# Mixer B's weights: 32x32 boxes turned by VectorE and placed through DRAM, in place of transposes on TensorE

## The chip, the cores and the metric

The kernel runs on one core of one Trainium2 chip. The metric is the device time in microseconds (us) of one execution, from start to end on that core; a lower time is better. Engines are named as the profile names them: PE (TensorE, matrix products), PEld (its loads of the stationary operand), DVE (VectorE), ACT (ScalarE), POOL (GpSimd) and SP (SyncE, which only issues DMAs; SPq is its queue).

## What is computed

One step of a layer with two attention mixers that work side by side on the same projection. 128 prompt tokens and 1024 latent tokens (eight tiles of 128) are normalized, projected and given rotary positions. Mixer A lets each latent token attend to all latent keys and 128 cached context keys. Mixer B lets it attend to the keys at most 128 places away, to the context keys, and to a learned sink per head. Each mixer has 8 query heads in two groups of four that share one key and value head of 64. The outputs are multiplied by SiLU gates, joined, and put through one output projection. What the change touches is mixer B for latent tokens:

```python
def window_attn_latent(q, k_lat, v_lat, k_ctx, v_ctx, sink):
    ...
    s_band = jnp.einsum('bnqkgd,bnskd->bnkgqs', qb, kband).astype(jnp.float32) * scale
    ...
    valid = (jnp.abs(rel)[None] <= WINDOW) & (abs_j >= 0) & (abs_j < n)
    s_band = jnp.where(valid[None, :, None, None], s_band, NEG_INF)
    s_ctx = jnp.einsum('bnqkgd,bskd->bnkgqs', qb, k_ctx).astype(jnp.float32) * scale
    ...
    s = jnp.concatenate([sink_column(sink, kv, s_ctx.shape[:-1]), s_ctx, s_band], axis=-1)
    p = jax.nn.softmax(s, axis=-1).astype(v_lat.dtype)
    ...
    o = (jnp.einsum('bnkgqs,bskd->bnqkgd', p_ctx, v_ctx)
         + jnp.einsum('bnkgqs,bnskd->bnqkgd', p_band, vband))
```

All of it is in float32. The kernel gets that precision from TensorE's fast format by splitting an operand into a high part and a low part, the rest that rounding left over, and adding the products.

## The kernel before

Projection, gates and keys come first; the last 400 us or so are the attention stage, and the change lies in it alone. The stage goes through 36 *units* in order: for latent tiles t = 1 to 8, for both groups g of heads, first mixer A (m = 0), then mixer B (m = 1); at the end four units of the prompt. An A unit and the B unit behind it are called a pair here.

Each unit is cut into *slots*, one for each block of 128 keys: nine for an A unit (context and eight tiles), and for a B unit four (the tile before, the context, the tile itself, the tile after; three for tiles 1 and 8, which lack a neighbour). The main loop at the end of the kernel takes the slots in order. In each, it first runs what was put on an agenda with `later(n, f)` (do f n slots from now), then `scores` of the slot's block, then what was due at this slot by plan (`put`), then two or three steps of the output projection, and last `values` of the block that is LAG = 3 slots back. `in_order` makes this written order the order of every engine's queue, SyncE's among them: an instruction that waits holds up all that stands behind it on its engine.

In an A unit, `scores` computes a block's scores already turned, keys on the partitions (L1316, L1317: bank st), ScalarE takes the exponential (L1319, pe) and its high part (L1323, ph), GpSimd or VectorE the low part (pl, L1327 or L1325). `values` multiplies both with the values (L1337, L1339, L1340: bank pv). The maxima that the exponentials need were found by L985 and L986 (pmx, mx).

A B unit i needs its scores with queries on the partitions, since the window's mask and the maximum go along the keys. `weight_items` does this early: in slots 0 to 3 of the A unit ahead, one head per slot, two matmuls (L1066, L1067: bank sn) and a VectorE instruction (L1070) that adds the mask and takes the minimum of the negated scores; one slot later ScalarE's exponential (L1056) writes the head's 128 x 512 weights to the tile `pen`. The weights are not divided; the sum's inverse is folded into the gates later (`sinks`, `total`, `divide`, `turned`, `put`, `rows`). `pen` has one buffer.

For `values` the weights have to be turned, keys on the partitions. In the B unit's slots, `scores` does this with four transposes on TensorE for each block (L1311, bank st), then ScalarE's copy (L1312, ph) and VectorE's subtraction (L1313, pl). For tiles 2 to 7 (`paired`) blocks 0 and 3 share one group of four transposes, because the window masks of the two leave complementary triangles: `pair` merges block 3 into block 0 (L1017 on VectorE) and leaves block 3 its diagonal (L1018 on GpSimd), the slot before the unit starts `unpair` turns the merged block (L1030, bank st_pair) and takes block 0 out of it (L1032), and `unpair_rest` takes out block 3 (L1036). Blocks 0 and 3 then get their high part from SBUF (L1304, ScalarE) and their low part on GpSimd (L1305).

SyncE's queue in a pair holds, in this order (slots counted from the start of the A unit): the rows of inverse sums of the pair before (L1134, slot 0), in every other pair a store of y (L1435, about slot 2), a gate (L1291, sgl) and a query tile (L965, qt) in slot 4, again a store of y, a gate and a query tile in slot 8, the inverse sums (L1129) and a query tile's part (L990, qb) in slot 10, and in the pairs that come before a store of y two loads of yt.

Of the kernel before, what the change touches and what calls it, by code (L numbers as in the profile page):

```python
# [12 lines left out]
I16 = mybir.dt.int16  # L13
# [6 lines left out]
P = 128  # L20
# [56 lines left out]
PAIR_AT = 2  # L77
# [40 lines left out]
def hybrid_step(ctx, tc, x_prompt, x_sample, cache_k_a, cache_v_a, cache_k_b, cache_v_b,  # L118
# [11 lines left out]
    gate_row = dram.tile([2, D], F32, name="gate_row")  # L130
    r_dram = [dram.tile([4, P], F32, name=f"rd{i}") for i in range(2 * NL)]
# [877 lines left out]
    divided = {}  # L1009

    def paired(t):

        return 1 < t < NL

    def pair(i):
        prev, nxt = (penat[i][:, :, o : o + P] for o in (0, 3 * P))
        nc.vector.copy_predicated(prev, mask[:, 0:P].bitcast(I16).unsqueeze(1).to_broadcast([P, 4, P]), nxt)  # L1017
        nc.gpsimd.affine_select(out=nxt, in_=nxt, pattern=[[0, 4], [-1, P]], compare_op=ALU.is_equal, fill=0.0, base=0,  # L1018
                                channel_multiplier=1)

    shared = {}

    def unpair(i):

        divided.pop(i)()
        prev = penat[i][:, :, 0:P]
        over = mask[:, 3 * P : 4 * P].unsqueeze(1).to_broadcast([P, 4, P])
        s = bank("B", f"st{i}_pair")
        for h in range(4):
            nc.tensor.transpose(s[:, P * h : P * h + P], prev[:, h], ident_r.bitcast(F32))  # L1030
        shared[i] = s.rearrange("p (h n) -> p h n", h=4)
        nc.vector.scalar_tensor_tensor(prev, over, 0.0, shared[i], op0=ALU.is_ge, op1=ALU.mult)  # L1032

    def unpair_rest(i):
        over = mask[:, 3 * P : 4 * P].bitcast(I16).unsqueeze(1).to_broadcast([P, 4, P])
        nc.vector.copy_predicated(penat[i][:, :, 3 * P : 4 * P], over, shared.pop(i))  # L1036

    def weight_items(i):
# [7 lines left out]
        def first(n):  # L1046
            if t:
                penat[i] = qp2[0].tile([P, 4, 512], F32, tag="pen", name=f"pen{i}")[:, :, 0:n]
            else:
                penat[i] = w3.tile([P, 512], F32, tag="pe", name=f"pen{i}", bufs=PES).rearrange(  # L1050
                    "p (h n) -> p h n", h=4)
# [3 lines left out]
        def exp(h, s, scale):  # L1055
            nc.scalar.activation(penat[i][:, h], s, AF.Exp, bias=v["nm"][:, h : h + 1], scale=scale,  # L1056
                                 accum_out=v["sum"][:, h : h + 1])

# [28 lines left out]
        def finish():  # L1087
            nc.gpsimd.tensor_tensor(v["ex"], v["nm"], sink[:, 4 * g : 4 * g + 4], op=ALU.add)
            if paired(t):
                later(PAIR_AT, lambda: pair(i))  # L1090
            if paired(t):
                later(EX_AT[0], sinks)
                later(EX_AT[1], total)
                divided[i] = divide
            elif t:
# [13 lines left out]
        def divide():  # L1109
# [6 lines left out]
            o = int(paired(t))  # L1116
            later(ROWS_AT[0] + o, turned)
            later(ROWS_AT[1] + o, put)
            later(ROWS_AT[2] + o, rows)
            later(ROWS_AT[3] + o, lambda: nc.gpsimd.tensor_tensor(sgl[i], sgl[i], v["rows"], op=ALU.mult))  # L1120
# [176 lines left out]
    def scores(i, b, blk):  # L1297
# [3 lines left out]
        if m == 1 and paired(t) and blk[0] in (0, 3):  # L1301
            p = penat[i][:, :, P * blk[0] : P * blk[0] + P]
            ph4, pl4 = (a.rearrange("p (h n) -> p h n", h=4) for a in (ph, pl))
            nc.scalar.copy(ph4, p)  # L1304
            nc.gpsimd.tensor_tensor(pl4, p, ph4, op=ALU.subtract)  # L1305
            return ph, pl
# [23 lines left out]
    def values(i, b, last, blk, ph, pl):  # L1330
# [15 lines left out]
        def inverse():  # L1346
            if t:
                v["rs"] = w2.tile([64, 512], F32, tag="rs", name=f"rs{i}", bufs=1)
            else:
                if not rs_prompt:  # L1350
                    rs_prompt.append(qp2[0].tile([P, 4, 512], F32, tag="pen", name="rs_prompt"))
                v["rs"] = rs_prompt[0][0:64, 2 * g + m]
# [6 lines left out]
        def gated():  # L1359
# [3 lines left out]
            pvv = pv[0:64, :].rearrange("p (c s n) -> p c s n", s=2, n=P)  # L1363
# [214 lines left out]
```

## Time and profile before

| | us |
|---|---|
| Time, median of 3 runs | 695.06 (694.6 to 695.15) |
| The profiled execution, its own time | 694.65 |
| Its span in the trace | 692.9 |
| PE busy | 686.3 |
| PEld busy | 555.2 |
| DVE busy | 470.6 |
| ACT busy | 407.2 |
| POOL busy | 379.9 |

How to read the profile: a line of a group names the source line, engine, operation, tiles (out<-in), shapes and count, then the busy time in us and the mean duration of one in ns, then the idle time of the engine just before them and what ended it. In a timeline the columns are start, duration (both us), engine, line, operation, tiles, shapes and count. Consecutive matmuls overlap in the pipeline, so their durations are longer than the distance from one start to the next. A DMA line gives the count, the size of one, and the median time from issue to landing.

### The profile page before, as it was taken

The page shows a single profiled execution, that of the slowest core. Times are in us where ns is not written, and L with a number is a line of the kernel's source. Part 1 is how long each engine was busy: PE and PEld are TensorE (multiplying, and loading weights), DVE is VectorE, ACT ScalarE, POOL GpSimd, SP SyncE. Part 2 cuts the span into 40 slices and gives each one's busy share as a digit, 9 for nine tenths or more (in the row PEclk, how much of TensorE's full clock was granted, in tenths as well). Part 3 has the DMA queues.
Part 4 walks back from the last instruction along what each step waited for, and adds up shares of the span by engine and source line. Part 5 has one row for each costly group of instructions (what it writes and reads, how often), then busy time and mean ns, then how long its engine had stood idle before and what let it go on. Part 6 is the DMA issues. An engine that isn't in the chain of part 4 may idle for free.

```text
span 692.9 us, 10678 instructions
## 1 busy us (share of the span) xinstructions
PE 686.3 (99%) x3493; PEld 555.2 (80%) x3493; DVE 470.6 (68%) x1025; ACT 407.2 (59%) x848; POOL 379.9 (55%) x392
## 2 busy tenths in 40 slices
PE   9999999999999999999999999999999999999997
PEld 4679988878788889987878888888887888887876
DVE  4775257968778764857778578676776776675563
ACT  5665412412322433189777887787778778877770
POOL 3556023233323330269687777877786778685751
PEclk9999999999999999999999999999999999999999
DMA  8971283349434016432222121222221221212323
GB/s 350 404 249 62 79 309 77 91 135 279 117 91 140 15 63 190 151 104 72 76 71 89 45 90 54 67 64 77 68 78 39 80 80 46 85 56 91 102 74 122
DMA packets 54231, 78.50 MB, mean 113 GB/s; under 512 B 6952, under 2 KB 25496, under 8 KB 54176
## 3 DMA queue, kind: packets, MB, share of 16 engines
q1 hardware_dynamic: 45936, 65.86, 28.9%
q10 hardware_dynamic: 8240, 11.96, 6.4%
q8 instruction: 27, 0.44, 0.3%
q14 instruction: 28, 0.23, 0.1%
HBM read 58.63 MB, written 19.18 MB: 112 GB/s over the span
## 4 chain that ended last, share of the span: by engine, by line
PE 96%; ACT 1%; DMA 1%; DVE 1%; POOL 0%; issue 0%; SPq 0%; ACTq 0%; POOLq 0%; DVEq 0%
PE po L1418 14%; PE pv L1340 7%; PE pv L1337 7%; PE pmx L985 5%; PE st L1316 5%; PE st L1317 5%; PE pv L1339 5%; PE pq L268 5%; PE pq L266 5%; PE pq L267 5%; PE pg L280 3%; PE pg L276 3%; PE pg L281 3%; PE pk L267 2%; PE pk L268 2%; PE pk L266 2%
## 5 line engine op out<-in xcount | busy, mean ns | idle before, releaser
L1327 POOL TENSOR_TENSOR pl<-pe,ph 128x512 fp32r<-128x512 f32 x130 | 167.4, 1297 | 62.3 <-ACT ph L1323 49.5
L986 DVE TENSOR_REDUCE mx<-pmx 128x1 f32<-128x384 f32 x192 | 100.9, 551 | 42.0 <-PE pmx L985 40.2
L1319 ACT ACTIVATE pe<-st 128x512 f32<-128x512 f32 x146 | 86.7, 594 | 23.8 <-PE st L1317 22.7
L1323 ACT CAST ph<-pe 128x512 fp32r<-128x512 f32 x146 | 90.7, 621 | 5.5
L1337 PE MATMUL pv<-ph,v_hi 128*128 128x512 f32 x208 | 83.4, 401 | 0.1
L1340 PE MATMUL pv<-pl,v_hi 128*128 128x512 f32 x208 | 82.2, 395 | 0.3 <-DVE pl L1313 0.2
L184 POOL TENSOR_TENSOR rs_q<-ms_q,mhalf 128x8 f32<-128x8 f32 x18 | 34.1, 1897 | 80.8 <-DVE ms_q L182 80.8
L1070 DVE CUSTOM_DVE_ANT_0 sn<-sn,mask,nsink 128x512 f32<-128x512 f32 (+1 forms) x64 | 46.3, 724 | 44.1 <-PE sn L1067 41.7
L1418 PE MATMUL po<-wo,ogh 128*128 128x512 f32 (+1 forms) x224 | 73.4, 388 | 0.0
L985 PE MATMUL pmx<-kha,qt 128*128 128x384 f32 x192 | 59.6, 357 | 0.2 <-DVE mx L986 0.2
L1339 PE MATMUL pv<-ph,v_lo 128*64 128x512 f32 x146 | 57.7, 395 | 0.0
L1317 PE MATMUL st<-qb,kla 68*128 68x512 f32 x144 | 57.3, 398 | 0.0
L1316 PE MATMUL st<-qt,kha 128*128 128x512 f32 x144 | 57.1, 397 | 0.0
L1340 PEld LDWEIGHTS pv<-pl,v_hi 128*128 128x128 f32 x208 | 39.1, 188 | 17.8 <-POOL pl L1327 0.6
L1056 ACT ACTIVATE pen<-sn,nm 128x512 f32<-128x512 f32 (+2 forms) x72 | 44.9, 625 | 6.6 <-DVE nm L1070 3.2
L1418 PEld LDWEIGHTS po<-wo,ogh 128*128 128x128 f32 x224 | 41.0, 188 | 6.3 <-ACT ogh L1380 0.3
L1337 PEld LDWEIGHTS pv<-ph,v_hi 128*128 128x128 f32 x208 | 39.2, 188 | 8.1 <-issue 0.6
L1305 POOL TENSOR_TENSOR pl<-pen,ph 128x512 fp32r<-128x512 f32 x24 | 30.9, 1288 | 25.2 <-PE pv L1337 22.9
L744 ACT CAST qo0q<-ptq 128x512 fp32r<-128x512 f32 x18 | 10.6, 586 | 57.2 <-PE ptq L741 53.7
L1418 PE MATMUL po<-wo,ogl 128*128 128x512 f32 (+1 forms) x112 | 43.5, 389 | 0.0
L985 PEld LDWEIGHTS pmx<-kha,qt 128*128 128x128 f32 x192 | 35.3, 190 | 7.7 <-DVE mx L986 1.2
L466 POOL TENSOR_TENSOR h<-hf,h 128x256 fp32r<-128x256 f32 (+2 forms) x32 | 27.4, 876 | 20.0 <-ACT h L460 10.0
(260 smaller groups left out, 1762.1 us busy)
## 6 DMA issues: line engine op xcount, KB each, us to landing
qt<-qd SPq DMA_DIRECT2D x36, 256.0 KB, 3.0
wm<-in_w_mod_ss_dram SPq DMA_DIRECT2D x7, 1024.0 KB, 11.4
qd<-qo0q ACTq DMA_DIRECT2D x36, 128.0 KB, 2.4
qd<-qo1q ACTq DMA_DIRECT2D x36, 128.0 KB, 2.4
sgl<-gd SPq DMA_DIRECT2D x35, 128.0 KB, 2.5
out_dram<-yt SPq DMA_DIRECT2D x17, 256.0 KB, 2.1
xn<-in_x_sample_dram SPq DMA_DIRECT2D x8, 512.0 KB, 6.2
wg<-in_w_mod_g_dram SPq DMA_DIRECT2D x4, 1024.0 KB, 8.4
```

Source lines behind the costliest of these rows:

```text
L266: nc.tensor.matmul(out, h_at(0, i, k, tok), w.hi[k], start=(k == 0), stop=False)
L985: nc.tensor.matmul(pm[:, 0:384], lhs, kha[:, g, 3 * b : 3 * b + 3, :], start=True, stop=True)
L986: nc.vector.tensor_reduce(mx[:, h, b : b + 1], pm[:, 0:384], axis=AX.X, op=ALU.max)
L1316: nc.tensor.matmul(s, kh, qtile[i], start=True, stop=False)
L1317: nc.tensor.matmul(s, kl, qbtile[i], start=False, stop=True)
L1319: nc.scalar.activation(pe, s, AF.Exp)
L1323: nc.scalar.copy(ph, pe)
L1327: nc.gpsimd.tensor_tensor(pl, pe, ph, op=ALU.subtract)
L1337: nc.tensor.matmul(pv, two, ph, start=(b == 0), stop=False)
L1339: nc.tensor.matmul(pv[0:64, :], vl, ph, start=False, stop=False)
L1340: nc.tensor.matmul(pv, two, pl, start=False, stop=last)
L1418: nc.tensor.matmul(po[n, q.start], a, wo_parts[KT * n + k][lo][:, q], start=(k == KS[0] and p == 0), stop=(k == KS[-1] and p == 2))
```

## The change

It is made for all B units of tiles 2 to 8 (`boxed`), 14 units; those of tile 1 and the prompt's keep TensorE's transposes. Gone are `pair`, `unpair` and `unpair_rest`, and for these units the transposes of `scores`: 48 in the shared groups, 96 for blocks 1 and 2 of tiles 2 to 7, and 24 for tile 8, 168 in all.

In their place, ScalarE's exponential writes a head's weights so that the boxes of 32 x 32 of the four heads lie interleaved: two halves (heads 0 and 1, heads 2 and 3), in each half the four quarters of a block's keys, in a quarter the blocks, in a block the two heads, and of a head 32 columns. One slot after the exponential, VectorE turns all boxes of the head in place with one instruction (`turn_boxes`). After the second head of a half, SyncE writes the half to DRAM (512 KB; 384 KB for tile 8), and `BOX_BACK` = 2 slots later reads it back with four DMAs (`fetch`), one for each quarter of the partitions, in runs of 1 KB, with the boxes in their turned places. So per unit there are four turns, two writes and eight reads, and in the written order: turn 0 in slot 2, turn 1 and the first write in slot 3, turn 2 in slot 4, the first four reads, then turn 3 and the second write in slot 5, the last four reads in slot 7, counted from the start of the A unit.

`scores` then only splits: the high part is ScalarE's copy out of SBUF for all blocks, the low part GpSimd's for blocks 0 and 2 and, a slot later, VectorE's for blocks 1 and 3. The columns come out in another order of queries and heads, which `gated` undoes. The inverse sums follow one slot earlier against `divide`, which itself comes one slot later than before for tiles 2 to 7.

```diff
--- before.py
+++ after.py
@@ -74,7 +73,7 @@
 PROMPT_LEAD = 4
 EX_AT = (2, 2, 5)
 ROWS_AT = (1, 1, 4, 6)
-PAIR_AT = 2
+BOX_BACK = 2
 KV_ORDER = [0] + list(range(1, NT))
 GATE_AT = (3, 7)
 QUERY_LAST = (0, 1, 2, 5)
@@ -128,6 +127,7 @@
     q_dram = [[dram.tile([P, 1024], F32, name=f"qd{t}_{m}") for m in range(2)] for t in range(NT)]
     g_dram = dram.tile([16 * HD, TOK], F32, name="gd")
     gate_row = dram.tile([2, D], F32, name="gate_row")
+    t_dram = [[dram.tile([P, 1024], F32, name=f"td{i}_{c}") for c in range(2)] for i in range(2)]
     r_dram = [dram.tile([4, P], F32, name=f"rd{i}") for i in range(2 * NL)]
 
     agenda = {}
@@ -1006,34 +1006,9 @@
                 out.append(lambda h=h, b=b: item(h, b))
         return out, finish
 
-    divided = {}
-
-    def paired(t):
-
-        return 1 < t < NL
-
-    def pair(i):
-        prev, nxt = (penat[i][:, :, o : o + P] for o in (0, 3 * P))
-        nc.vector.copy_predicated(prev, mask[:, 0:P].bitcast(I16).unsqueeze(1).to_broadcast([P, 4, P]), nxt)
-        nc.gpsimd.affine_select(out=nxt, in_=nxt, pattern=[[0, 4], [-1, P]], compare_op=ALU.is_equal, fill=0.0, base=0,
-                                channel_multiplier=1)
-
-    shared = {}
-
-    def unpair(i):
-
-        divided.pop(i)()
-        prev = penat[i][:, :, 0:P]
-        over = mask[:, 3 * P : 4 * P].unsqueeze(1).to_broadcast([P, 4, P])
-        s = bank("B", f"st{i}_pair")
-        for h in range(4):
-            nc.tensor.transpose(s[:, P * h : P * h + P], prev[:, h], ident_r.bitcast(F32))
-        shared[i] = s.rearrange("p (h n) -> p h n", h=4)
-        nc.vector.scalar_tensor_tensor(prev, over, 0.0, shared[i], op0=ALU.is_ge, op1=ALU.mult)
-
-    def unpair_rest(i):
-        over = mask[:, 3 * P : 4 * P].bitcast(I16).unsqueeze(1).to_broadcast([P, 4, P])
-        nc.vector.copy_predicated(penat[i][:, :, 3 * P : 4 * P], over, shared.pop(i))
+    def boxed(t):
+
+        return t > 1
 
     def weight_items(i):
 
@@ -1045,7 +1020,12 @@
 
         def first(n):
             if t:
-                penat[i] = qp2[0].tile([P, 4, 512], F32, tag="pen", name=f"pen{i}")[:, :, 0:n]
+                flat = qp2[0].tile([P, 2048], F32, tag="pen", name=f"pen{i}")[:, 0 : 4 * n]
+                if boxed(t):
+                    v["flat"] = flat
+                    penat[i] = flat.rearrange("p (e k x) -> p k e x", e=8, x=64)
+                else:
+                    penat[i] = flat.rearrange("p (h n) -> p h n", h=4)
             else:
                 penat[i] = w3.tile([P, 512], F32, tag="pe", name=f"pen{i}", bufs=PES).rearrange(
                     "p (h n) -> p h n", h=4)
@@ -1053,8 +1033,33 @@
                 v[x] = small(x)
 
         def exp(h, s, scale):
-            nc.scalar.activation(penat[i][:, h], s, AF.Exp, bias=v["nm"][:, h : h + 1], scale=scale,
+            to = penat[i][:, h] if not boxed(t) else boxes(h).rearrange("p b k j -> p k b j")
+            if boxed(t):
+                s = s.rearrange("p (k b j) -> p k b j", b=4, j=32)
+            nc.scalar.activation(to, s, AF.Exp, bias=v["nm"][:, h : h + 1], scale=scale,
                                  accum_out=v["sum"][:, h : h + 1])
+            if boxed(t):
+                later(1, lambda: turn_boxes(h))
+
+        def boxes(h):
+            return v["flat"].rearrange("p (c b k s j) -> p c s b k j", c=2, b=4, s=2, j=32)[:, h // 2, h % 2]
+
+        def turn_boxes(h):
+
+            nc.vector.transpose(boxes(h), boxes(h))
+            c, s = divmod(h, 2)
+            if s == 0:
+                return
+            n = v["flat"].shape[1] // 2
+            half = v["flat"][:, n * c : n * c + n]
+            td = t_dram[i // 2 % 2][c][:, 0:n]
+            nc.sync.dma_start(td, half)
+            later(BOX_BACK, lambda: fetch(half, td))
+
+        def fetch(half, td):
+            for b in range(4):
+                nc.sync.dma_start(half[32 * b : 32 * b + 32].rearrange("p (a x) -> p a x", a=4),
+                                  td.rearrange("(a j) (b x) -> b j a x", a=4, b=4)[b])
 
         def item(h):
             p0, p1_ = window(t)
@@ -1086,13 +1091,7 @@
 
         def finish():
             nc.gpsimd.tensor_tensor(v["ex"], v["nm"], sink[:, 4 * g : 4 * g + 4], op=ALU.add)
-            if paired(t):
-                later(PAIR_AT, lambda: pair(i))
-            if paired(t):
-                later(EX_AT[0], sinks)
-                later(EX_AT[1], total)
-                divided[i] = divide
-            elif t:
+            if t:
                 for n, f in zip(EX_AT if i > 3 else EX_EARLY, (sinks, total, divide)):
                     later(n, f)
             else:
@@ -1113,11 +1112,10 @@
                     nc.vector.tensor_scalar(penat[i][:, h], penat[i][:, h], v["inv"][:, h : h + 1], None, op0=ALU.mult)
                 return
 
-            o = int(paired(t))
-            later(ROWS_AT[0] + o, turned)
-            later(ROWS_AT[1] + o, put)
-            later(ROWS_AT[2] + o, rows)
-            later(ROWS_AT[3] + o, lambda: nc.gpsimd.tensor_tensor(sgl[i], sgl[i], v["rows"], op=ALU.mult))
+            later(ROWS_AT[0], turned)
+            later(ROWS_AT[1], put)
+            later(ROWS_AT[2], rows)
+            later(ROWS_AT[3], lambda: nc.gpsimd.tensor_tensor(sgl[i], sgl[i], v["rows"], op=ALU.mult))
 
         def turned():
             v["pt"] = bank("A", f"pti{i}")[0:4, 0:P]
@@ -1298,11 +1296,14 @@
 
         t, m, g = units[i]
         ph, pl = parts_tiles(i, b)
-        if m == 1 and paired(t) and blk[0] in (0, 3):
-            p = penat[i][:, :, P * blk[0] : P * blk[0] + P]
-            ph4, pl4 = (a.rearrange("p (h n) -> p h n", h=4) for a in (ph, pl))
+        if m == 1 and boxed(t):
+            p = penat[i][:, blk[0]]
+            ph4, pl4 = (a.rearrange("p (e x) -> p e x", e=8) for a in (ph, pl))
             nc.scalar.copy(ph4, p)
-            nc.gpsimd.tensor_tensor(pl4, p, ph4, op=ALU.subtract)
+            if blk[0] % 2:
+                later(1, lambda: nc.vector.tensor_tensor(pl4, p, ph4, op=ALU.subtract))
+            else:
+                nc.gpsimd.tensor_tensor(pl4, p, ph4, op=ALU.subtract)
             return ph, pl
         s = bank("B", f"st{i}_{b}")
         if m == 1:
@@ -1348,8 +1349,8 @@
                 v["rs"] = w2.tile([64, 512], F32, tag="rs", name=f"rs{i}", bufs=1)
             else:
                 if not rs_prompt:
-                    rs_prompt.append(qp2[0].tile([P, 4, 512], F32, tag="pen", name="rs_prompt"))
-                v["rs"] = rs_prompt[0][0:64, 2 * g + m]
+                    rs_prompt.append(qp2[0].tile([P, 2048], F32, tag="pen", name="rs_prompt"))
+                v["rs"] = rs_prompt[0][0:64, 512 * (2 * g + m) : 512 * (2 * g + m) + 512]
             if m == 1:
                 (nc.vector.tensor_copy if i < 4 else nc.scalar.copy)(v["rs"], pv[64:128, :])
                 return
@@ -1360,10 +1361,11 @@
             rs = v["rs"]
             o = 768 + 256 * (i % 3)
             of = spare[:, o : o + 256].rearrange("p (c n) -> p c n", c=2)
-            pvv = pv[0:64, :].rearrange("p (c s n) -> p c s n", s=2, n=P)
-            srv = rs.rearrange("p (c s n) -> p c s n", s=2, n=P)
+            a = 4 if m and boxed(t) else 1
+            pvv, srv = (x.rearrange("p (c a s n) -> p s c a n", c=2, a=a, s=2) for x in (pv[0:64, :], rs))
+            ofv = of.rearrange("p c (a n) -> p c a n", a=a)
             for s in range(2):
-                nc.vector.tensor_tensor(of[64 * s : 64 * s + 64], pvv[:, :, s, :], srv[:, :, s, :],
+                nc.vector.tensor_tensor(ofv[64 * s : 64 * s + 64], pvv[:, s], srv[:, s],
                                         op=ALU.add if m else ALU.mult)
             nc.gpsimd.tensor_tensor(of, of, sgl.pop(i), op=ALU.mult)
             later(GATE_LATE, lambda: load_gate(i + 2 + (i + 2 >= APART)))
@@ -1475,11 +1477,6 @@
         for s, f in zip(at, items):
             put(s, f)
         put(end, done)
-
-    for i, (t, m, g) in enumerate(units):
-        if m and paired(t):
-            put(start[i] - 1, lambda i=i: unpair(i))
-            put(start[i], lambda i=i: unpair_rest(i))
 
     for k, at in enumerate(HELD):
         put(at, lambda k=k: held_gates(k))
```

More of the change, by code (lines that the diff above doesn't have):

```diff
@@ L12 @@
 BF16 = mybir.dt.bfloat16
-I16 = mybir.dt.int16
 AF = mybir.ActivationFunctionType
```

## Prediction

> **What bounds the kernel now.** I read the page first: busy time by engine, and the chain that ended last.
>
> ```profile
> PE 686.3 (99%) x3493; PEld 555.2 (80%) x3493; DVE 470.6 (68%) x1025; ACT 407.2 (59%) x848; POOL 379.9 (55%) x392
> ...
> PE 96%; ACT 1%; DMA 1%; DVE 1%; POOL 0%; issue 0%; SPq 0%; ACTq 0%; POOLq 0%; DVEq 0%
> ```
>
> TensorE is nearly always busy and makes up 96% of the chain, so a microsecond taken from it is a microsecond of the total, as long as its operands still come in time. A mean over the span can hide a stage with another limit, so next the windows over two pairs of units (A then B) of the stage that changes; columns are the stretch, its length, and the busy time of PE, weight loads, DVE, ACT and POOL, then the granted clock.
>
> ```profile
> 405.00:428.00 23.00, 23.00 (x111) 18.46 (x110) 17.34 (x37) 17.92 (x38) 17.21 (x18) 1.00 0.23 72
> 428.00:452.00 24.00, 24.00 (x115) 19.36 (x114) 16.11 (x35) 19.01 (x39) 18.11 (x19) 1.00 0.22 68
> ```
>
> TensorE has no idle time here, at the full granted clock (1.00); ACT, DVE and POOL are busy about 70 to 80% of a pair. So the pair is as long as its TensorE work.
>
> **What leaves TensorE.** "Busy" can't price a pipelined instruction: the distance from start to start can. The PE timeline over one pair:
>
> ```profile
> 428.16 0.39 PE L1316 MATMUL st<-qt,kha 128*128 128x512 f32 x1
> ...
> 444.42 0.52 PE L985 MATMUL pmx<-kha,qt 128*128 128x384 f32 x2
> 444.79 0.60 PE L1030 MATMUL st_pair<-ident_r,pen 128*128 128x128 f32 x4
> 445.14 0.48 PE L1337 MATMUL pv<-ph,v_hi 128*128 128x512 f32 x1
> 445.46 0.40 PE L1339 MATMUL pv<-ph,v_lo 128*64 128x512 f32 x1
> 445.69 0.40 PE L1340 MATMUL pv<-pl,v_hi 128*128 128x512 f32 x1
> 445.93 0.34 PE L985 MATMUL pmx<-kha,qt 128*128 128x384 f32 x1
> 446.10 0.39 PE L1337 MATMUL pv<-ph,v_hi 128*128 128x512 f32 x1
> ...
> 446.90 0.60 PE L1311 MATMUL st<-ident_r,pen 128*128 128x128 f32 x4
> 447.26 0.42 PE L985 MATMUL pmx<-kha,qt 128*128 128x384 f32 x1
> 447.52 0.40 PE L1337 MATMUL pv<-ph,v_hi 128*128 128x512 f32 x1
> ...
> 448.22 0.60 PE L1311 MATMUL st<-ident_r,pen 128*128 128x128 f32 x4
> 448.57 0.60 PE L985 MATMUL pmx<-kha,qt 128*128 128x384 f32 x2
> 449.01 0.62 PE L1418 MATMUL po<-wo,ogh 128*128 128x512 f32 x2
> ...
> 451.13 0.39 PE L1337 MATMUL pv<-ph,v_hi 128*128 128x512 f32 x1
> 451.36 0.40 PE L1340 MATMUL pv<-pl,v_hi 128*128 128x512 f32 x1
> ```
>
> Four transposes hold the engine 0.35 us (444.79 to 445.14), 0.36 and 0.35. What follows them is late as well: L1337 takes 0.32 to the next start where 0.23 is usual (445.46 to 445.69), the single L985 0.26 where 0.17 is usual (445.93 to 446.10), the two L985 0.44 where 0.37 is usual (444.42 to 444.79). A group therefore costs 0.44, 0.45 and 0.42: 1.31 us for each B unit. The 168 transposes are 42 groups in 14 units (tiles 2 to 8, two units each; tile 8 has no shared group but three of its own, priced the same): 14 x 1.31 = **18.3 us**. The bounds: 42 x 0.35 = 14.7 without the followers' share; above, nothing but the row of the group's mean, a rival below.
>
> **What the other engines get.** The groups by shape:
>
> ```profile
> L1311 PE MATMUL st<-ident_r,pen 128*128 128x128 f32 x152 | 22.8, 272 | 0.1
> ...
> L1032 DVE SCALAR_TENSOR_TENSOR pen<-mask,st_pair 128x512 f32<-128x512 bf16 x12 | 7.9, 656 | 0.0
> L1017 DVE COPY_PREDICATED pen<-mask,pen 128x512 f32<-128x512 int16 x12 | 9.2, 769 | 0.4
> L1036 DVE COPY_PREDICATED pen<-mask,st_pair 128x512 f32<-128x512 int16 x12 | 8.8, 734 | 0.0
> L1018 POOL TENSOR_SCALAR_AFFINE_SELECT pen<-pen 128x512 f32<-128x512 f32 x12 | 7.6, 631 | 0.0
> ...
> L1325 DVE TENSOR_TENSOR pl<-pe,ph 128x512 fp32r<-128x512 f32 x16 | 11.1, 693 | 21.1 <-POOL ogl L1383 16.1 <-ACT ph L1323 5.0
> L1305 POOL TENSOR_TENSOR pl<-pen,ph 128x512 fp32r<-128x512 f32 x24 | 30.9, 1288 | 25.2 <-PE pv L1337 22.9 <-ACT ph L1304 2.3
> ```
>
> No box transpose is in this trace. The nearest row is L1325, the same 512 floats a partition from SBUF to SBUF in 0.69 us; I take that. It can't be free, and twice (1.38) is the other end. A paired unit then adds 4 x 0.69 = 2.76 to VectorE and takes away 0.66 + 0.77 + 0.73 = 2.16: +0.6 of 17, while POOL loses 0.63. Each unit keeps two low parts on POOL (1.29 each) and two on VectorE; tile 8's two units move two each to POOL, busy far less than the span. ScalarE's exponentials and copies keep their sizes and change only strides; I cost them at nothing, covered by the 5 us that ScalarE is idle in a pair. A PSUM bank is freed, which no wait in the trace asks for. Throughput thus allows the 18.3.
>
> **The new wait.** Where an exponential went straight to TensorE, it now makes a round trip: VectorE turns head 1, SyncE's queue writes half 0 (512 KB) to DRAM, waits until it has landed, issues four 128 KB reads, only then writes half 1, waits again, issues four more. ScalarE's copy of block 0 needs all eight, as each block crosses both halves and all partitions. In the queue's written order the store of y (if any) stands ahead of the first write, the loads of sgl and qt between it and the first reads; they issue while it is in flight. Behind the last reads stand y, sgl, qt, the row sums and qb, each wanted slots later. The rows for it, in the same pair and, in the second fence, the pair before with its store of y:
>
> ```profile
> 433.36 0.76 DVE L1070 CUSTOM_DVE_ANT_0 sn<-sn,mask,nsink 128x512 f32<-128x512 f32 x1 [0.69 <-PE sn L1067]
> 434.14 0.08 DVE L1070 DVE_READ_ACCUMULATOR2_ANT nm<- 128x1 f32 x1
> 437.71 0.19 ACT L1056 ACTIVATION_READ_ACCUMULATOR pen<-sn,nm 128x1 f32 x1
> 446.57 0.62 ACT L1304 CAST ph<-pen 128x512 fp32r<-128x512 f32 x1 [0.70 <-DVE pen L1032]
> ```
>
> ```profile
> 404.62 0.39 PE L1316 MATMUL st<-qt,kha 128*128 128x512 f32 x1
> 411.34 0.69 DVE L1434 TENSOR_TENSOR yt<-po,yt 128x512 f32<-128x512 f32 x1
> 412.06 0.35 SPq L1435 DMA_DIRECT2D out_dram<-yt  x1
> 447.74 0.47 SPq L990 DMA_DIRECT2D qb<-qd  x1
> ```
>
> ```profile
> qt<-qd SPq DMA_DIRECT2D x36, 256.0 KB, 3.0
> ...
> out_dram<-yt SPq DMA_DIRECT2D x17, 256.0 KB, 2.1
> ...
> wraw<-in_w_out_dram SPq DMA_DIRECT2D x16, 256.0 KB, 4.1
> ...
> qb<-qd SPq DMA_DIRECT2D x18, 128.0 KB, 2.7
> ```
>
> A 256 KB store lands 2.1 us after issue; 128 KB more cost 0.3 (qb against qt), so 512 KB: 2.1 + 0.6 = 2.7. A 128 KB read: 2.7, like qb. An issue: 0.47, with its gap 0.5. The trip is 2.7 (write) + 2.0 (four issues) + 2.7 (write) + 1.5 + 2.7 (last read), plus 0.1 for each of five hand-overs (an estimate; the y store follows its add by 0.03): **12.1 us**. Half 1 is never what it waits for: its last exponential ends at 437.90, turned by about 438.6, while the queue reaches that write at 434.9 + 4.9 = 439.8.
>
> The start is VectorE's turn of head 1, written behind head 2's mask-and-maximum: 434.22 + 0.69 = 434.9, 6.75 us after the pair's first score matmul (428.16). In a pair that stores y its two operations are ahead too: 412.03 + 0.69 = 412.7, 8.1 us after 404.62. So block 0 has landed 18.85 or 20.2 us into the pair; with the copy (0.62) and POOL's subtraction (1.29) its low part is ready at **20.8 or 22.1**. TensorE wanted it at 451.36 - 428.16 = 23.2, and with 1.31 taken out before that, at **21.9**. Half the pairs have 1.1 us to spare; the other half (tiles 2 to 8 have one of each) wait 0.2. The other blocks come with the same reads. ScalarE, which takes its queue in order, picks block 0 up at 18.85 to 20.2 instead of 18.4 (446.57): up to 1.8 us later, which its idle time works off before the next head's exponential is turned.
>
> The sum: 18.3 - 7 x 0.2 = **16.9 us**. The profiled execution took 694.65 (span 692.9), 0.41 under the median of 695.06; against the median, **678.2**.
>
> [...]
>
> **The rivals.**
> 1. *The round trip becomes the bound: slower.* For it: the slack is 1.1 us on one sort of pair and none on the other, two writes and two reads stand one behind the other in one queue, and a 256 KB transfer among others took 4.1 us (wraw). With 4.1 for each write the trip is 2.8 longer; the pairs wait 3.0 and 1.7: 7 x 4.7 = 32.9 - 18.3 = 14.6 lost, **709.7**. It turns from gain to loss when the trip is 1.76 us too long (7 x 1.96 + 7 x 0.66 = 18.3). Against it: in this stage the DMA engines are 22% busy (windows), and qt's 256 KB takes 3.0 there. Chance 0.20; another 0.05 that it lands at that point, no change.
> 2. *Some of it given back.* The trip is 1 us longer, or a turn costs 1.38: then head 0's and head 1's turns put the start 1.4 later. Waits of 1.2 and 0, or 1.6 and 0.3: 8.4 or 13.3 lost, **685.2 to 690.1**. Chance 0.22.
> 3. *The transposes cost TensorE what their mean says.* 168 x 0.272 = 45.7 us, **649.4**. Against it: the timeline, where four start within 0.36. Chance 0.02. [...]
> 4. *The change doesn't bring its overlap,* as the heads' interleaved boxes lie in one another's address range, and exponentials wait for turns. Against it: at 446.90 TensorE reads block 1 while VectorE rewrites block 3 of the same rows, interleaved by head. It would hold ScalarE 1.4 us twice and end as rival 2; in its chance.
>
> **How the numbers follow.** The forecast, 676 to 682, has 0.51; with rivals 2 and 3, faster 0.75. Unchanged, within 0.2% (1.4 us, about what a measurement of this kernel can tell from no change), 0.05; slower 0.20. The range: below, the whole 18.3 without a wait is 676.8, with 1.8 for small things 675; above, it reaches into rival 1 as far as 701, leaving out about 0.13 there and 0.05 below.
>
> **What would show it.** Right: L1030 gone and L1311 down to 32; pairs of about 22.3 us where 23.5 were (428.16 less 404.62); VectorE turns near 0.7 us; writes landing in about 2.7, reads in 2.7; idle TensorE, if any, at pv of block 0, only in pairs that store y. Wrong: PE waiting there in every pair, released by ScalarE's copy or POOL's low part, with SyncE's queue waiting for its own writes.

## The result and the profile after

| | before | after |
|---|---|---|
| Median, 6 runs each on the same chip | 694.93 us (694.6 to 695.15) | 734.66 us (726.64 to 736.64) |
| Profiled execution: own time, span | 694.65, 692.9 | 736.0, 734.0 |
| Span less PE's busy time | 6.6 | 39.5 |

The ratio is 1.0549 [1.0494, 1.0604]: slower by 5.5%, and outside the predicted range. The page of the changed kernel, with its busy times, its chain, the two subtractions of the boxed blocks and the two DMA groups of the round trip:

```profile
PE 694.5 (95%) x3325; PEld 545.8 (74%) x3325; DVE 485.3 (66%) x1041; ACT 406.2 (55%) x848; POOL 376.9 (51%) x384
...
PE 72%; DMA 9%; DVE 7%; ACT 3%; issue 3%; POOL 3%; SPq 2%; ACTq 0%; POOLq 0%; DVEq 0%
...
L1306 POOL TENSOR_TENSOR pl<-pen,ph 128x512 fp32r<-128x512 f32 x28 | 41.1, 1485 | 25.7 <-ACT ph L1302 18.3
L1304 DVE TENSOR_TENSOR pl<-pen,ph 128x512 fp32r<-128x512 f32 x26 | 25.6, 983 | 35.4 <-ACT ph L1302 25.2
...
td<-pen SPq DMA_DIRECT2D x24, 512.0 KB, 3.2
pen<-td SPq DMA_DIRECT2D x96, 128.0 KB, 2.9
```

The 168 matmuls are gone (3493 less 3325), yet PE is busy for 8.2 us longer, and TensorE's part of the chain falls from 96% to 72%. Two neighbouring pairs as windows, in the columns used before (stretch, length, busy time of PE, PEld, DVE, ACT, POOL, granted clock):

```profile
441.90:467.70 25.80, 23.28 (x100) 17.62 (x99) 16.15 (x34) 18.34 (x37) 17.03 (x17) 0.99 0.46 140
467.70:495.90 28.20, 25.43 (x100) 19.17 (x100) 19.33 (x39) 18.34 (x37) 17.04 (x17) 0.90 0.42 135
```

A pair was 23.5 us long with no idle TensorE. Now TensorE idles 2.5 and 2.8 us in it, and in the second its clock is at 0.90. What it waited for in the attention stage (line, releaser: total us, times, longest), and what SyncE's queue waited for:

```profile
PE pmx L985 <- ACT spare L1126: 21.2, 12, 3.2
PE ptm L999 <- DVE mx L986: 6.0, 10, 0.6
PE pmx L985 <- DVE mx L986: 2.3, 10, 0.2
```

```profile
SPq L1056 <- DVE pen L1049: 64.1, 14, 11.0
SPq L1061 <- DMA td<-pen: 58.8, 27, 3.7
```

Nothing here names a weight of mixer B (pv), where the prediction looked for the wait. TensorE waits for a bank: the maximum of a later A unit (pmx) needs bank A's buffer, and that is held by the turned inverse sums (pti) until ScalarE has copied them out (L1126). The copy is a quarter of a microsecond long and its input had been ready for 3.8 us (486.53 to 490.31). It stood in ScalarE's queue behind the copy of block 0 (L1302), which waited for the round trip. The timelines of SyncE, ScalarE and TensorE in the second pair (start, duration, engine, line, and in brackets the idle time before and its releaser):

```profile
475.65 0.33 SPq L1056 DMA_DIRECT2D td<-pen  x1
...
478.74 1.74 SPq L1061 DMA_DIRECT2D pen<-td  x4
480.58 0.38 SPq L1056 DMA_DIRECT2D td<-pen  x1
484.19 2.82 SPq L1061 DMA_DIRECT2D pen<-td  x4
```

```profile
484.83 0.62 ACT L1324 CAST ph<-pe 128x512 fp32r<-128x512 f32 x1
489.79 0.62 ACT L1302 CAST ph<-pen 128x512 fp32r<-128x512 f32 x1 [4.34 <-DMA out_dram<-yt]
490.31 0.25 ACT L1126 COPY spare<-pti 4x128 f32<-4x128 f32 x1
```

```profile
486.26 0.27 PE L1122 MATMUL pti<-ident_r,inv 128*4 128x128 f32 x1
...
487.46 0.44 PE L985 MATMUL pmx<-kha,qt 128*128 128x384 f32 x1
490.62 0.69 PE L985 MATMUL pmx<-kha,qt 128*128 128x384 f32 x1 [2.71 <-ACT spare L1126]
```

ScalarE's row names a store of y as the releaser. A wait is put down to what came last by the profile, and the store was issued right behind the reads; what the copy reads are the eight reads' bytes, the last of them issued by 487.01, 2.8 us before it starts. And the clock over the same idle stretch:

```profile
482.00:488.00 6.00, 5.85 (x25) 3.78 (x23) 4.51 (x10) 2.75 (x5) 4.48 (x4) 1.00 0.49 154
488.00:490.60 2.60, 0.00 (x0) 0.00 (x0) 0.00 (x0) 0.81 (x3) 0.11 (x1) 0.88 0.70 212
490.60:497.00 6.40, 6.38 (x16) 4.84 (x17) 3.96 (x6) 2.64 (x5) 2.85 (x2) 0.51 0.22 75
497.00:500.00 3.00, 3.00 (x14) 2.44 (x13) 1.51 (x5) 2.82 (x6) 1.30 (x1) 1.00 0.00 0
```

TensorE idles 2.6 us and then works 6.4 us at a granted clock of 0.51: 16 matmuls in 6.4 us, where 14 took 3.0 behind it. So this wait costs its own length and then about as much again. That is why PE's busy time grew while its work shrank.

### The profile page after: what moved, and what is told of

Its sections match the earlier page's. It is cut to its first block, busy times and chain, and to the rows that moved or that the text cites. A ratio compares the mean times of both kernels' runs of the same rounds, so it can differ in the third digit from the quotient of the medians.

```text
span 734.0 us, 10592 instructions
## 1 busy us (share of the span) xinstructions
PE 694.5 (95%) x3325; PEld 545.8 (74%) x3325; DVE 485.3 (66%) x1041; ACT 406.2 (55%) x848; POOL 376.9 (51%) x384
## 4 chain that ended last, share of the span: by engine, by line
PE 72%; DMA 9%; DVE 7%; ACT 3%; issue 3%; POOL 3%; SPq 2%; ACTq 0%; POOLq 0%; DVEq 0%
PE po L1420 10%; PE pq L268 4%; PE pq L266 4%; PE pq L267 4%; PE pv L1341 4%; PE pv L1338 4%; PE st L1318 3%; PE st L1317 3%; DMA sgl<-gd 3%; PE pmx L985 3%; PE pg L280 3%; PE pg L276 3%; PE pg L281 3%; DMA td<-pen 2%; PE pk L267 2%
## 5 line engine op out<-in xcount | busy, mean ns | idle before, releaser
L985 PE MATMUL pmx<-kha,qt 128*128 128x384 f32 x192 | 66.3, 381 | 24.0 <-ACT spare L1126 21.2
L1341 PE MATMUL pv<-pl,v_hi 128*128 128x512 f32 x208 | 84.6, 407 | 0.4 <-POOL pl L1328 0.2
L1420 PE MATMUL po<-wo,ogh 128*128 128x512 f32 (+1 forms) x224 | 77.3, 407 | 0.0
L985 PEld LDWEIGHTS pmx<-kha,qt 128*128 128x128 f32 x192 | 36.8, 192 | 45.8 <-ACT spare L1126 24.3
L1302 ACT CAST ph<-pen 128x512 fp32r<-128x512 f32 x54 | 31.9, 613 | 43.5 <-DMA sgl<-gd 23.7
L1306 POOL TENSOR_TENSOR pl<-pen,ph 128x512 fp32r<-128x512 f32 x28 | 41.1, 1485 | 25.7 <-ACT ph L1302 18.3
L1304 DVE TENSOR_TENSOR pl<-pen,ph 128x512 fp32r<-128x512 f32 x26 | 25.6, 983 | 35.4 <-ACT ph L1302 25.2
L1420 PEld LDWEIGHTS po<-wo,ogh 128*128 128x128 f32 x224 | 43.6, 200 | 7.0 <-ACT ogh L1382 0.3
L1420 PE MATMUL po<-wo,ogl 128*128 128x512 f32 (+1 forms) x112 | 45.4, 405 | 0.0
```

The source lines that it names most:

```text
L985: nc.tensor.matmul(pm[:, 0:384], lhs, kha[:, g, 3 * b : 3 * b + 3, :], start=True, stop=True)
L1341: nc.tensor.matmul(pv, two, pl, start=False, stop=last)
L1420: nc.tensor.matmul(po[n, q.start], a, wo_parts[KT * n + k][lo][:, q], start=(k == KS[0] and p == 0), stop=(k == KS[-1] and p == 2))
```

## The experiments

Every kernel was timed against the kernel before on the same chip; the medians of before were 695.28, 695.37, 695.49 and 695.22 in the four groups, and the time of the changed kernel is 734.66 throughout. The first three experiments ask which of two things makes the loss: the length of the trip, or what is queued behind it.

**e1: the change without its trip.** Left out: all writes and reads, so the turned boxes stay where they are and the output of mixer B is not the reference's.

```diff
-            nc.sync.dma_start(td, half)
-            later(BOX_BACK, lambda: fetch(half, td))
```

> Leaves out the writes to DRAM and the reads back: the boxes are turned but stay where they are, so mixer B's weights for tiles 2 to 8 are in wrong places. Everything else is as in the changed kernel. Theory A (the loss is all the round trip: ScalarE's copy of block 0 waits for the reads, and what stands behind it in ScalarE's queue holds TensorE): without the trip TensorE waits as little as in the kernel before, and the 18.3 us of transposes come out: 677, between 675 and 681, granted clock 1.00 throughout. Theory B (VectorE's turns and the low parts, which now take 0.98 us on VectorE and 1.49 on GpSimd where 0.69 and 1.29 were, cost a good part of it): above 690, with TensorE waiting for VectorE or GpSimd.

Measured: 687.6 us (686.74 to 692.32), ratio 0.9905 [0.987, 0.9939]. The page, and what TensorE's weight loads for the maxima waited for:

```profile
PE 673.8 (98%) x3325; PEld 535.8 (78%) x3325; DVE 482.3 (70%) x1041; ACT 406.7 (59%) x848; POOL 377.3 (55%) x384
```

```profile
PEld pmx L985 <- DVE mx L986: 12.8, 45, 0.5
```

The trip costs 47 us, more than the whole loss. But without it only 7.7 us come out, not some 18. The first pair of tile 8 goes from 21.04 to 19.64 us (first score matmul to first score matmul), near the 1.31 that was priced; the pairs of tiles 3 to 7 only from about 23.47 to 22.75. There the maxima wait for VectorE in 45 small stretches; before there were 4, with 1.2 us. The time lies between what theory A and theory B expect.

**e2: the inverse sums ahead of block 0's copy.**

```diff
-EX_AT = (2, 2, 5)
+EX_AT = (2, 2, 4)
```

> The inverse sums are taken one slot earlier, so that ScalarE's small copy of their transpose (which frees the PSUM bank that TensorE's next maxima go to) stands ahead of the copy of block 0 in ScalarE's queue, not behind it. The round trip is as it was. Theory A (that order makes TensorE wait about two slots earlier than the weights are needed): TensorE's waits for that copy, 21 us in 12 places, go; the next late thing is block 0's low part at pv, 1.1 us late in pairs without a store of y and 2.1 in pairs with one, so 7 x 3.2 - 18.3 = 4 over the kernel before: about 699, 690 to 710, and the stretches at half the clock go or get fewer. Theory C (the trip bounds the pair wherever the wait is met): the wait moves to pv at its full size and the time stays at 725 to 737.

Measured: 741.65 us (739.45 to 743.04), ratio 1.0665 [1.0644, 1.0686], slower still, and above what either theory allowed. The wait for ScalarE's small copy is down to 2.1 us, and in its place stands, as the largest of PE's waits,

```profile
PE ptm L999 <- DVE mx L986: 30.3, 12, 6.1
```

That is the same wait one engine further on. VectorE's low part of block 1 (L1304) waits for ScalarE's copy of block 1, and the maxima that TensorE needs next stand behind it in VectorE's queue.

**e3: the reads one slot later,** so that the second write goes out ahead of the first reads.

```diff
-BOX_BACK = 2
+BOX_BACK = 3
```

> The reads of a half are written one slot later in SyncE's queue, so that the second half's write no longer stands behind the first half's reads and its wait for the first write. Theory A: the second write goes out 1.5 to 2 us earlier, block 0 comes that much earlier, and TensorE's wait for ScalarE's small copy falls from about 2.7 us a pair to about 1; the stretches at half the clock go: 700 to 712. Theory D (DRAM or the DMA engines are what is slow, not the order in the queue): the second write lands later for it, block 0 comes no earlier, 728 to 740.

Measured: 736.84 us (736.12 to 739.97), ratio 1.0608 [1.0584, 1.0631]: no gain, in the range of theory D, but not for its reason. The second write did go out earlier (2.5 us behind the first in the pairs that store y, where it was 4.9), but the last reads now fall in slot 8 and stand behind that slot's store of y, which waits for VectorE. PE's largest wait is the old one:

```profile
PE pmx L985 <- ACT spare L1126: 24.8, 8, 4.0
```

**e4: e2 and e3 together.**

> The two edits together. Theory A: block 0's low part is due when TensorE wants it, within 0.3 us: 677 to 686, faster than the kernel before. Theory C or D: not below 700.

Measured: 745.97 us (744.24 to 749.96), ratio 1.0722 [1.0704, 1.074], the worst of all; the maxima's wait (ptm for mx) is 35.5 us in 12 stretches. The two edits only moved the wait along the queues. What had to move was either the waiting instruction itself or the end of the trip, without setting the reads behind the store.

**e5: another order in SyncE's queue.** The second write goes out ahead of the first reads, and the last reads follow one slot behind them, ahead of the store.

```diff
-            later(BOX_BACK, lambda: fetch(half, td))
+            if c == 0:
+                v["back"] = half, td
+                return
+            fetch(*v["back"])
+            later(1, lambda: fetch(half, td))
```

> SyncE's queue in another order: second write, then the first half's four reads at once, then (one slot later, ahead of any store of y) the second half's four reads. So the second write no longer waits for the first, and no read stands behind a store of y, as the reads did in the kernel with the later reads. Theory E (in-order queues: block 0's copy must start by about 19 us into a pair, as ScalarE's, VectorE's and GpSimd's other work stands behind the split; the trip's length in the queue decides): the last reads land at about 19.4 instead of 21 to 22, TensorE's idle time in a pair falls below 1 us, no stretch at half the clock: 688 to 702. Theory D (DRAM and DMA engines are slow however they are asked): 725 to 740.

Measured: 709.53 us (707.45 to 710.1), ratio 1.0202 [1.0183, 1.022]: 25 us better than the change, but not as good as expected. The trip, from the first write's issue to ScalarE's copy of block 0, is 12.0 us on average over the 12 pairs of tiles 2 to 7 (11.1 to 12.9), where the change has 13.5 (13.0 to 14.2). ScalarE and VectorE still wait in their queues. ScalarE, VectorE and TensorE at the end of one pair (in edited kernels the line numbers shift by a few: L1306 is the change's L1302, L1308 its L1304):

```profile
501.23 0.62 ACT L1306 CAST ph<-pen 128x512 fp32r<-128x512 f32 x1 [1.15 <-DMA sgl<-gd]
```

```profile
502.56 1.38 DVE L1308 TENSOR_TENSOR pl<-pen,ph 128x512 fp32r<-128x512 f32 x1 [0.81 <-ACT ph L1306]
503.87 1.01 DVE L986 TENSOR_REDUCE mx<-pmx 128x1 f32<-128x384 f32 x2
```

```profile
504.47 0.22 PE L999 MATMUL ptm<-ident_r,m_nat 128*4 128x128 f32 x1 [0.80 <-DVE mx L986]
```

The copy is 1.15 us late; VectorE's low part idles 0.81 for the next copy and takes 1.38, where the pair's last one takes 0.68 (in the changed kernel's trace the long ones are those that began during a GpSimd subtraction, last section), the two reductions behind it start only then, and TensorE waits 0.80 for them. It is a chain of short waits now, through three queues in order.

**e6: the splits one slot later.** Each boxed block's copy and low part are issued a slot behind the block's own, so that they stand behind the small copy and the maxima; `values` is three slots back and still gets them in time. SyncE's order is the change's.

```diff
-            nc.scalar.copy(ph4, p)
-            if blk[0] % 2:
...
+            def split():
+                nc.scalar.copy(ph4, p)
+                if blk[0] % 2:
...
+            later(1, split)
```

> The trip is as in the changed kernel, but each block of the boxed units is split (ScalarE's copy, then the low part) one slot later than its turn, still one to two slots before TensorE multiplies with it. Theory E: what counts is where the splits stand in the in-order queues, not when TensorE needs the block; with the small copy, the maxima's reductions and the slot's other work ahead of them, TensorE's waits at the maxima and their transpose go, and what is left is block 0's low part 0.6 to 1.6 us late at pv: 695 to 715. Theory T (the trip ends too late for TensorE's use of the block, wherever the split stands): the wait moves to pv in full, 728 to 745.

Measured: 702.25 us (701.66 to 704.89), ratio 1.011 [1.0088, 1.0132], as expected. 32 of the 40 us that were lost come back although the trip is as long as in the change (12.6 to 14.1): TensorE's long waits for the small copy are gone. The largest that is left stands where the prediction looked for it, at pv, behind GpSimd's low part:

```profile
PE pv L1345 <- POOL pl L1308: 5.6, 7, 0.9
```

**e7: e5 and e6 together.**

> Both: the better order in SyncE's queue and the splits one slot later. Theory E: the trip is hidden and the time is that of the kernel without the trip, 686 to 693, faster than the kernel before. Theories D and T: above 710.

Measured: 687.62 us (685.7 to 689.27), ratio 0.9891 [0.9866, 0.9916]: faster than before by 7.7 us, and equal to e1, which makes no trip at all. All the writes and reads are there and cost nothing.

**e8: the traffic without the need.** As the change, but the reads go to another place in DRAM and nobody waits for them. Left out: the weights are not put in place, so the output of mixer B is not the reference's.

```diff
-            later(BOX_BACK, lambda: fetch(half, td))
+            later(BOX_BACK, lambda: fetch(f_dram[i // 2 % 2][c][:, 0:n], td))
```

> The changed kernel with the reads' target moved from the tile to another place in DRAM: the same writes and reads, in the same order in SyncE's queue, but no engine waits for the reads (mixer B's weights for tiles 2 to 8 stay in wrong places). Theory E (only the wait costs, not the traffic): 686 to 692, as without the trip. Theory D (the traffic or the full queue delays other loads, or slows the engines): above 700, with TensorE waiting for loads or for work that waited for them.

Measured: 725.34 us (723.19 to 729.94), ratio 1.0442 [1.0394, 1.049]: theory E misses by more than 30 us, and theory D (the traffic or the full queue) has the right side. Nobody needs these reads, and yet they cost 38 us over e1. TensorE's largest wait, SyncE's queue in one pair, and TensorE's wait at the start of the next pair:

```profile
PE st L1319 <- DMA qb<-qd: 25.4, 13, 3.4
```

```profile
421.88 0.33 SPq L1057 DMA_DIRECT2D td<-pen  x1
...
424.95 2.49 SPq L1062 DMA_DIRECT2D fd<-td  x4
427.53 0.54 SPq L1057 DMA_DIRECT2D td<-pen  x1
431.18 2.45 SPq L1062 DMA_DIRECT2D fd<-td  x4
...
435.87 0.49 SPq L991 DMA_DIRECT2D qb<-qd  x1
```

```profile
439.69 0.47 PE L1319 MATMUL st<-qb,kla 68*128 68x512 f32 x1 [2.56 <-DMA qb<-qd]
```

The query's tail rows (qb) for the next A unit stand in SyncE's queue behind two writes and eight reads, 14 us behind the first write. Twice the queue's reads wait for a write to land: they go out 3.07 and 3.65 us after its issue. The changed kernel has the same block in its queue, but no wait for qb is among its larger ones; that its TensorE comes later for other waits would explain it, which was not tested.

**e9: e8's traffic in e5's order.** The same part is left out.

> The kernel of e8 (the reads go to another place in DRAM and nobody waits for them, so the weights stay in their wrong places) with the DMA order of e5: the second write goes out ahead of the first reads, the last reads one slot later. Theory Q (order in SP's queue: in e8 TensorE waited 25.4 us in 13 stretches for the DMA of the query's tail rows of the next A unit, which stands in SP's queue behind both pairs of write and reads, each of which holds the queue until its write has landed, 3.0 to 3.6 us): with one wait fewer the tail rows go out some 4 us earlier, TensorE finds them, and the time is that of the kernel without the trip, 686 to 692 us. Theory T (the 28 MB of added traffic itself slows the loads that TensorE needs): the bytes are the same as in e8, so it stays above 715 us.

Measured: 689.51 us (687.83 to 689.91), ratio 0.9906 [0.9889, 0.9922], as the queue's order has it. SyncE's queue in a pair of the same sort, with stores of y:

```profile
458.86 0.33 SPq L1057 DMA_DIRECT2D td<-pen  x1
...
461.35 0.32 SPq L1057 DMA_DIRECT2D td<-pen  x1
461.94 5.36 SPq L1067 DMA_DIRECT2D fd<-td  x8
...
470.47 0.50 SPq L991 DMA_DIRECT2D qb<-qd  x1
```

The tail rows go out 11.6 us behind the first write instead of 14.0. The bytes are the same and 36 us are gone, so it wasn't the traffic.

**e10 and e11: one maximum moved out of mixer B's middle slot,** in e7, to slot 6 or to slot 4 of the A unit.

```diff
-MX_AT = (-4, -3, -2, -2, -1, 4, 5, 5, 7, 7, 8, 8)
+MX_AT = (-4, -3, -2, -1, 4, 5, 5, 6, 7, 7, 8, 8)
```

> e7 (both edits) with one of the two maxima of mixer B's middle slot moved to slot 6 of the A unit, which holds none. Theory M (of the 1.31 us that the transposes take in a pair, the part that doesn't come out, about 0.3, is bank A's maxima waiting for VectorE's reductions in B's shortened slots: 8.8 us in 33 waits of PEld in e7): pairs go from 22.5 to about 22.25 us, 14 pairs, so 683 to 686 us. Theory N (a transpose group takes less of TensorE than 0.44 us, and nothing is left to come out): 687 to 689 us. If slot 6 has no room on VectorE, over 690 us.

> As e10, but the maximum goes to slot 4 of the A unit, which holds one. Theory M: 683 to 686 us. Theory N: 687 to 689 us. If slot 4, the first after the four score rows of mixer B, has no room in bank A, over 690 us.

Measured: 688.18 us (686.9 to 690.03), ratio 0.9895 [0.9877, 0.9913], for slot 6, nothing against e7; and 701.25 us (698.61 to 703.43), ratio 1.0079 [1.0052, 1.0106], for slot 4. There the maximum finds bank A still held by ScalarE's exponential of the last score row, PE's largest wait in e11:

```profile
PE pmx L985 <- ACT pen L1039: 7.1, 7, 1.5
```

So the rest of the gain does not hang on that one slot. Nor did e10 take away what it was to test: the weight loads of the maxima wait 9.5 us for VectorE in it, where e7 has 8.8.

**e12: e7, with the last boxed unit split in its own slots.**

```diff
-            later(1, split)
+            later(1, split) if i < PROMPT_AT - 1 else split()
```

> e7, but the splits of the last unit of mixer B before the prompt's (its blocks are exponentials of tile 8) run in their own slots, as in the changed kernel. In e7's profile TensorE has one long idle stretch behind that unit: 3.1 us, in which VectorE's scaling of the prompt's exponentials takes 2.4 us, and the clock is at half for 6.8 us about it. Theory K (the late split puts ScalarE's and VectorE's work of the last block beside the prompt's, and an idle stretch of 3 us costs as much again in half clock): idle falls under 2 us and the half clock there goes: 682 to 685.5 us. Rival: the last unit's blocks, split in their own slots, hold ScalarE's and VectorE's queues as in e5, and the pair behind it loses what the prompt gains: 687 to 691 us.

Measured: 684.75 us (684.31 to 686.29; before 695.22), ratio 0.9856 [0.9839, 0.9873], the fastest version. The windows of e7, then of e12, over the idle stretch behind that unit and the work after it:

```profile
651.20:654.30 3.10, 0.01 (x2) 0.01 (x1) 2.66 (x6) 1.18 (x3) 2.26 (x4) 0.92 0.01 2
654.30:661.00 6.70, 6.70 (x24) 5.73 (x25) 3.34 (x8) 2.78 (x11) 1.09 (x3) 0.53 0.03 8
```

```profile
650.60:652.50 1.90, 0.01 (x1) 0.01 (x1) 1.12 (x6) 1.71 (x4) 0.27 (x2) 1.00 0.04 13
652.50:659.00 6.50, 6.34 (x34) 5.05 (x35) 4.35 (x12) 5.15 (x17) 3.44 (x6) 1.00 0.14 40
```

The stretch is 1.2 us shorter, and 34 matmuls fit where 24 did: the granted clock behind it is 1.00, where e7 has 0.53. The length of an idle stretch alone does not tell whether the half clock comes: in the changed kernel's attention stage six of 1.84 to 3.20 us came with half clock, during them or within 2.2 us of their end, and three of 1.66, 1.71 and 2.25 did not. What brings it on was not shown. The same kernel can also meet it or not: two of e7's four executions have a mean granted clock of 0.999 and took 685.7 and 686.5 us, within 0.2 us of e12's range, so what e12 gains on e7 shows only against the other two (0.995 and 0.997, 689.3 and 688.8 us).

## Why the prediction was wrong, point by point

- **Transposes (18.3 us): the groups' own spacing held, the yield didn't.** In the pairs of tiles 3 to 7 the twelve transposes filled 1.07 us from start to start, as read (0.35, 0.36 and 0.35), and in e12 the pairs are 1.0 shorter (23.47 to 22.47). Of the followers' share (0.25 in a pair) nothing came out in sum: the L1337 behind the shared group is back at 0.23, but in the B unit two of the maxima's matmuls now take 0.25 and 0.28 to the next start where 0.17 is usual, and the matmul ahead of the first of them 0.34 for 0.23. The weight loads of these two wait for VectorE's reductions (0.21 and 0.26 in one pair). The first pair of tile 8 gave 1.39 (21.04 to 19.65; 1.31 forecast), but the first of tile 2 gave nothing (22.29 to 22.64), and the stretch from the last pair's start to the end grew by 1.9 (56.0 to 57.9), so the span fell by 9.7 us (692.9 to 683.2). No run here took the maxima's waits away, so what a pair would be without them is not shown.
- **VectorE's turn (0.69 us): right.** 48 of them took 708 ns on average. **Start (6.75 or 8.1 us into the pair): right.** 475.65 is 7.9 us into its pair, which starts at 467.74; the pair before, without a store, has 6.7.
- **The trip (12.1 us): mis-sized by 1 to 2 us.** In the pair shown the first write landed in 3.1 us and the second in 3.6 (478.74 less 475.65, 484.19 less 480.58; 2.7 forecast for each), the first four issues took 1.8 (2.0), and from the first of the last four reads to the copy it was 5.6 (1.5 + 2.7 = 4.2), as one issue stalled for 1.5 us. Together 14.1. No run shows a term that the forecast's upper end, 682, would come from; in its place stand the medians of the changed kernel, 3.2 us for a write of 512 KB and 2.9 for a read of 128 KB.
- **The low parts (0.69 us on VectorE, 1.29 on GpSimd): mis-sized.** They took 0.98 and 1.49 on average: VectorE's took 0.68 with nothing on GpSimd and 1.24 when they began during a GpSimd subtraction (last section).
- **The step that failed** is the sentence on ScalarE: "picks block 0 up at 18.85 to 20.2 instead of 18.4 (446.57): up to 1.8 us later, which its idle time works off before the next head's exponential is turned". It counted the engine's idle time and the block's own due time at pv. It didn't list what stood behind the copy in ScalarE's queue, nor behind the low part in VectorE's. For SyncE's it did ("y, sgl, qt, the row sums and qb, each wanted slots later"), but e8 shows that qb was wanted sooner than it came. The small copy that frees bank A was wanted by TensorE at 487.9, 20.2 us into the pair, 1.7 before the 21.9 that the forecast took for the limit. e5 comes nearest to a test of this step: its trip is 12.0 us and its copy starts 19.4 us into the pair on average, just what was forecast, and yet it takes 709.5, not 678.2. Taking the splits out of the way (e7) brings 22 of those 31 us; the other 9 are missing in e1 too, which makes no trip (687.6).
- **The clock.** The forecast had no term for it. The span grew by 41.1 us: idle time by 32.9 (6.6 to 39.5), PE's busy time by 8.2. The same matmuls are busy 673.8 us in e1, at full clock throughout, so 20.7 us of busy time were added, against 12.5 that the transposes gave. Most of it is half clock: the mean granted clock of 0.976 over 734 us alone makes 17.6. The kernel's six executions agree: at a mean clock of 0.990 it took 726.6 us, at 0.971 736.6.
- **Rival 1** (the round trip becomes the bound) had the right side, and rightly saw two writes and two reads behind one another in one queue. Its point of turning ("1.76 us too long") was wrong, as e5 loses 14 us with a trip of the length that was forecast, and its 709.7 was 25 us short, as it let TensorE wait at pv and at full clock. Traffic as such showed no cost here (e7 at 687.62 us and e9 at 689.51, against e1 at 687.6 with a range of 686.74 to 692.32).

Two orders thus make the loss: the one in SyncE's queue (mended in e5, 25 us) and the place of the splits in ScalarE's and VectorE's (mended in e6, 32 us). The two overlap: mending both (e7) brings 47, all that the trip costs, and the time of e1.

## What to carry to other kernels

When an operand begins to come later, go through the queue of every engine that will wait for it, and list what stands behind the waiting instruction and who needs that: the first need in that list is the deadline, not the operand's own use. In a queue with two write-and-read-back trips put both writes first (25 us in e5), and move a waiting instruction behind the short ones that others need (32 us in e6). On a TensorE that is nearly always busy, look at the granted clock behind every idle stretch: in the changed kernel's attention stage nine stretches of 1.7 to 3.2 us, 20.9 us together, went with 34 us at half clock, some 17 us lost.

## What the runs showed of the hardware that was not expected

- In the changed kernel a DMA's issue on SyncE had a median of 0.34 us for the writes of the halves, 0.43 for the read-backs and 0.47 for qt and qb, but single ones of the read-backs took 1.5 to 1.8. In e8 the reads from DRAM to DRAM took 0.6 each (four in 2.49 and in 2.45).
- VectorE's subtraction of a boxed block took 983 ns on average and GpSimd's 1485, where the same subtraction of 512 floats took 693 and 1288 before. In the changed kernel 12 of VectorE's 26 ran with nothing on GpSimd and took 682 ns on average, and the 14 that began during a GpSimd subtraction took 1242 and ended after it; the GpSimd subtractions that began during one of those took about 1715, where 1288 was the mean before. So the boxes' strides showed no cost here (682 against 693); the long ones are those with the other engine's subtraction beside them. What makes them long was not shown.
- A small copy of 0.25 us that stood behind a copy waiting for the round trip stopped TensorE for 21.2 us in all (12 times), more than the 18.3 us at which the 168 transposes were priced.
